# A 32-byte pad in place of a 160-byte one between the two stacks of on-chip buffers, in a decoder layer on one core

## The chip, the core and the metric

The kernel runs on one core of one Trainium2 chip. The time is the device time of one execution in microseconds (us); lower is better. The engines are named as the profile names them: PE (TensorE, matmuls), PEld (its weight loads), DVE (VectorE), ACT (ScalarE), POOL (GpSimd) and SP (SyncE, which issues most of the DMAs).

## The reference

One layer of a hybrid decoder, for 1024 tokens of width 1024 in float32:

```python
h = rms_norm(x, norm_mix_pre[l])
proj = h @ w_in[l]                        # RWKV-7 columns | S5 input | two gates
o_rwkv = rwkv7_branch(...) @ w_branch_rwkv[l]
o_s5 = s5_branch(...) @ w_branch_s5[l]
mixed = (g_rwkv * o_rwkv + g_s5 * o_s5) @ w_out[l]
x = x + rms_norm(mixed, norm_mix_post[l])
h = rms_norm(x, norm_ffn_pre[l])
f = conv_ffn(h, ffn_w_up[l], ..., ffn_w_down[l])   # up, causal conv of width 3, gelu(gate)*val, down
x = x + rms_norm(f, norm_ffn_post[l])
```

The RWKV branch is a delta-rule recurrence over time with a data-dependent decay; the S5 branch is a diagonal complex state-space scan.

## The kernel before

Every large product is done in three matmuls of 128x512 per block of 128 inputs: each float32 operand is split into a high part rounded to fp32r and a low part (the rest), and high*high, high*low and low*high are summed. In a matmul one operand is loaded into PE as weights (128x128, PEld's rows) and the other, of 128x512, is streamed through; "moving operand" below is the streamed one. In the profile's rows a matmul is written `out<-moving,weights`. There are three places in the code that issue such triples:

- `mm3_steps` (lines 173 to 175): input projection, gates, branch projections, output projection and the first up-projection units. The weights `wh`, `wl` (or `lx`) come from `load_w`, which has ACT cast a loaded tile `wf` (line 157) and DVE subtract (line 158). The moving operands are the split activations `hh`, `hl`, in one stage `e`, in another `t`, in a third `lx`.
- `product` (lines 1344 to 1346): the up-projection of the other units, by a Winograd-Strassen scheme of seven products. The weights are `h`, `l` (tags h0 to h2, l0 to l2) and for the seventh product `w`; the moving operands are `hh`, `hl` and `t`.
- `step` in `down` (lines 1518 to 1520): the down-projection, by seven products as well, with weights `wh`, `wl` and moving operands `xh`, `xl`.

PE runs in the order in which the code is written (a manual schedule for PE); background products fill the time in which the recurrences' short matmuls wait.

**Where the tiles lie.** On-chip buffers are taken from two stacks in each partition's bytes: pools opened as usual grow from the low end, pools with `side="right"` from the high end downwards. `pad` is the first thing on the right, so its size sets where everything else on the right begins. It is written once, by POOL (line 1653), and read by nothing. Nearly all large tiles are 2048 or 4096 bytes in a partition, so that on one side they have the same remainder by 512. In the two built programs these are (bytes within a partition, the lowest tile of each row; the left pool `rk` of the recurrence is the exception, at 320):

| tiles | side, pool | address before | mod 512 | address after | mod 512 |
|---|---|---|---|---|---|
| `wh`, `wl`, `wf` of load_w | left, wp | 25792 | 192 | 25792 | 192 |
| `h`, `l` of the up-projection's products | left, upz, ups, upr | 42176 | 192 | 42176 | 192 |
| `lx` (mixing), `t` of the second half's branch and output projections (`t2`) | left, lxp, work2 | 46272 | 192 | 46272 | 192 |
| `hh`, `hl` (both halves) | right, hp0, hp1 | 163648 | 320 | 163776 | 448 |
| `w` (h3, l3) of the seventh product | right, hp1 | 175936 | 320 | 176064 | 448 |
| `t` of the up-projection (topp) | right, topp | 98112 | 320 | 98240 | 448 |
| `e` (early), and the recurrence's `ar`, `bk`, `gr`, `mt` on the right | right, early, rka | 119616 | 320 | 119744 | 448 |
| `wh`, `wl`, `xh`, `xl`, `A`, `T` of the down-projection | right, dq0, dqf, dqt | 108352 | 320 | 108480 | 448 |
| `st`, `S`, `B` of the down-projection | left, dqs, dqa, dqb | 25792 | 192 | 25792 | 192 |

So before the change a right tile of the table lies 128 bytes off a left one, modulo 512 as modulo 256; after it, 256 bytes off modulo 512, and not at all modulo 256. 660 of the 2316 buffers are on the right.

Of the kernel before, what the change touches and what calls it, by code (L numbers as in the profile page):

```python
# [9 lines left out]
F32 = mybir.dt.float32  # L10
# [61 lines left out]
class Kern:  # L72
# [1558 lines left out]
    def build(self):  # L1631
        tc, nc = self.tc, self.nc
        with tc.tile_pool(name="const", bufs=1) as self.const, tc.tile_pool(name="small", bufs=1) as self.small, \
                tc.tile_pool(name="dram", bufs=1, space=DRAM) as self.dram:
            def dr(n, shape=(128, T)):
                return self.dram.tile(list(shape), F32, name=n)
            for n in ("TZ", "TA", "TG"):
                setattr(self, n, [dr(f"{n}{p}") for p in range(4)])
            self.GT = [dr(f"GT{m}") for m in range(16)]
            self.RKV = [dr(f"RKV{m}") for m in range(12)]  # L1640

            self.US = [dr(f"US{m}", (8, 16, 8, 128)) for m in range(4)]
            self.YU = [dr(f"YU{m}", (8, 16, 8, 128)) for m in range(4)]
            self.YR = [dr(f"YR{m}") for m in range(4)]
            self.X1 = dr("X1", (D, T))
            self.H0 = [dr(f"H0{k}", (128, 512)) for k in range(NK)]
            self.ACT = [dr(f"ACT{i}") for i in range(FT)]
            self.tail = self.flip = False
            psum = dict(bufs=1, space=PSUM)
            with tc.manual_schedule(engines={mybir.EngineType.PE}), \  # L1650
                    tc.tile_pool(name="pad", bufs=1, side="right") as pad:

                self.nc.gpsimd.memset(pad.tile([128, 40], F32, name="pad"), 0.0)
                with tc.tile_pool(name="hp0", bufs=1, side="right") as hp0, \
                        tc.tile_pool(name="hp1", bufs=1, side="right") as hp1, ExitStack() as tops:
                    self.hp = (hp0, hp1)
                    with ExitStack() as low:
                        self.wp = low.enter_context(tc.tile_pool(name="wp", bufs=1))
                        self.front_half()
                        self.tail = True  # L1660
                        self.ps = tops.enter_context(tc.tile_pool(name="psd", **psum))
                        self.nrm = low.enter_context(tc.tile_pool(name="nrm", bufs=1))
                        mx = []
                        with tc.tile_pool(name="work2", bufs=NT2B) as self.work:
                            self.mix_out(mx)
                        self.early_stack.close()
                        self.topp = tops.enter_context(tc.tile_pool(name="topp", bufs=1, side="right"))
                        self.y1p = low.enter_context(tc.tile_pool(name="y1p", bufs=1))
                        self.work = low.enter_context(tc.tile_pool(name="work3", bufs=NT2C))
                        self.y1, self.T = [None] * NK, [[] for _ in range(4)]  # L1670
                        self.fill, self.fill_prio = [self.first_units(0)], 0
                        self.drive([(HP2, self.mid_norms(1, mx))])
                        self.drain()
                        for j, _ in enumerate(self.parts(self.first_units(1), 4)):
                            self.prep_t(j)
                        begun = {}
                        for i in (NFIRST, NFIRST + 1):
                            wh, wl = self.load_w(self.a["w_up"][i])
                            begun[i] = self.begin(i, {n + 1: ((wh[n], wl[n]), 0) for n in range(2)})
                    with tc.tile_pool(name="upz", bufs=1) as upz, tc.tile_pool(name="ups", bufs=1) as ups, \  # L1680
                            tc.tile_pool(name="upr", bufs=1) as upr, tc.tile_pool(name="upy", bufs=1) as upy:
                        self.up = dict(zg=upz, zv=upz, h0=upz, s=ups, h1=ups, l1=ups, h2=ups, l2=ups, r1=upr, r2=upr,
                                       l0=upr, y=upy)
                        self.fast_up(begun)
                with ExitStack() as st:
                    def pool(n, **k):
                        return st.enter_context(tc.tile_pool(name=n, bufs=1, **k))
                    right = [pool(n, side="right") for n in ("dq0", "dqf", "dqt")]
                    left = [pool(n) for n in ("dqa", "dqs", "dqb")]
                    self.ps = pool("psw", space=PSUM)  # L1690
                    self.down(*right, *left)
# [212 lines left out]
```

## Time and profile before

| | |
|---|---|
| time, median of 3 runs | 1575.57 us (1574.95 to 1576.25) |
| the profiled execution's own time | 1576.7 us |
| its span, first to last instruction | 1574.9 us |
| PE busy | 1502.9 us, 95% of the span |
| DVE, ACT, POOL busy | 1127.4, 693.7, 165.5 us |
| mean granted TensorE clock | 0.98 |
| chain of work that ended last, by engine | PE 73%, DVE 14%, DMA 6%, issue 3%, ACT 3% |

PE's rows overlap each other: the end of a matmul is modelled, and the next one starts before it. How long a matmul keeps PE is therefore read from one start to the next, or from a stretch that PE fills wholly: its length by the number of weight loads in it, since each matmul has one.

### The profile page before, as it was taken

Reading aid. Unit: us, or ns where it says so; the run is one execution under the profiler, and the core shown is the slowest. Engines: PE = TensorE matmul, PEld = TensorE weight load, DVE = VectorE, ACT = ScalarE, POOL = GpSimd, SP = SyncE. Lnnn points to the kernel's source line nnn. Section 1 sums busy time; section 2 is a strip of 40 time slices with the busy share of each in tenths; the row PEclk is TensorE's granted clock in tenths of the full one; section 3 lists DMA queues with packets and bytes.
Section 4 is the critical chain, followed back from the end, with each engine's and each line's share of the span. In section 5 each row is a group of like instructions: output and inputs, shape, how many; then the busy total and the mean of one; then the engine's idle time right before and its main releaser. Section 6 shows DMA issues by size and latency. Waiting matters only on the chain.

```text
span 1574.9 us, 26064 instructions
## 1 busy us (share of the span) xinstructions
PE 1502.9 (95%) x10028; PEld 1193.0 (76%) x10028; DVE 1127.4 (72%) x1963; ACT 693.7 (44%) x1115; POOL 165.5 (11%) x218
## 2 busy tenths in 40 slices
PE   5999899999999999999998999999999999999995
PEld 4787788787777776667686888788888887888884
DVE  6798784664465666875586689877777777688777
ACT  5354442324243445554434445444444445443451
POOL 2120000515224132100000000000000000000000
PEclk9999999999999999999898999999999999999997
DMA  6164243344335256542764443322222224953722
GB/s 209 41 192 132 85 124 122 113 137 143 107 118 159 86 180 160 154 150 101 235 215 152 140 143 132 114 80 81 81 80 81 81 81 169 323 196 120 232 77 107
DMA packets 133421, 213.86 MB, mean 136 GB/s; under 512 B 38656, under 2 KB 44800, under 8 KB 133296
## 3 DMA queue, kind: packets, MB, share of 16 engines
q1 hardware_dynamic: 124208, 188.32, 36.1%
q0 software_dynamic: 7936, 21.77, 4.7%
q10 hardware_dynamic: 1152, 2.10, 0.3%
q8 instruction: 79, 1.29, 0.3%
q14 instruction: 46, 0.38, 0.1%
HBM read 156.56 MB, written 53.48 MB: 133 GB/s over the span
## 4 chain that ended last, share of the span: by engine, by line
PE 73%; DVE 14%; DMA 6%; issue 3%; ACT 3%; SPq 0%; POOL 0%; DVEq 0%; ACTq 0%; POOLq 0%
PE gm L173 10%; PE gm L174 9%; PE gm L175 9%; PE rp L1344 4%; PE rp L1345 4%; PE rp L1346 4%; DMA st<-in_w_down_dram 2%; PE mm L1346 2%; PE mm L1345 2%; PE mm L1344 2%; PE d L1519 2%; PE d L1520 2%; PE d L1518 2%; PE ch L173 2%; PE ch L174 2%
## 5 line engine op out<-in xcount | busy, mean ns | idle before, releaser
L173 PE MATMUL gm<-hh,wh 128*128 128x512 f32 x688 | 295.0, 429 | 5.3 <-ACT hh L227 2.1
L174 PE MATMUL gm<-hl,wh 128*128 128x512 f32 x688 | 273.6, 398 | 0.4 <-DVE hl L228 0.4
L175 PE MATMUL gm<-hh,wl 128*128 128x512 f32 x656 | 260.5, 397 | 0.0
L157 ACT CAST wh<-wf 128x512 fp32r<-128x512 f32 x179 | 110.6, 618 | 216.2 <-PE gm L174 131.0
L158 DVE TENSOR_TENSOR wl<-wf,wh 128x512 fp32r<-128x512 f32 x175 | 123.6, 707 | 102.8 <-ACT wh L157 95.4
L173 PEld LDWEIGHTS gm<-hh,wh 128*128 128x128 f32 x688 | 130.5, 190 | 43.6 <-issue 4.6
L174 PEld LDWEIGHTS gm<-hl,wh 128*128 128x128 f32 x688 | 131.5, 191 | 24.9 <-issue 1.4
L175 PEld LDWEIGHTS gm<-hh,wl 128*128 128x128 f32 x656 | 124.7, 190 | 29.6
L1518 PE MATMUL d<-xh,wh 128*128 128x512 f32 x308 | 120.8, 392 | 2.1 <-ACT xh L227 2.1
L1519 PE MATMUL d<-xl,wh 128*128 128x512 f32 x308 | 120.8, 392 | 1.9 <-DVE xl L228 1.9
L1520 PE MATMUL d<-xh,wl 128*128 128x512 f32 x308 | 120.5, 391 | 0.0
L1344 PE MATMUL rp<-t,h 128*128 128x512 f32 x216 | 85.5, 396 | 1.4 <-ACT p L1358 1.4
L1346 PE MATMUL rp<-t,l 128*128 128x512 f32 x216 | 85.3, 395 | 0.3 <-DVE l L228 0.3
L1345 PE MATMUL rp<-t,h 128*128 128x512 f32 x216 | 85.4, 395 | 0.0
L1519 PEld LDWEIGHTS d<-xl,wh 128*128 128x128 f32 x308 | 58.2, 189 | 15.1 <-DVE xl L228 3.2
L1518 PEld LDWEIGHTS d<-xh,wh 128*128 128x128 f32 x308 | 58.2, 189 | 14.6 <-ACT xh L227 2.4
L1520 PEld LDWEIGHTS d<-xh,wl 128*128 128x128 f32 x308 | 58.2, 189 | 12.2
L227 ACT CAST h<-r 128x1024 fp32r<-128x1024 f32 x34 | 35.7, 1050 | 63.4 <-PE rp L1345 33.9
L228 DVE TENSOR_TENSOR l<-r,h 128x1024 fp32r<-128x1024 f32 x34 | 41.7, 1225 | 30.3 <-ACT h L227 28.9
L1365 DVE SCALAR_TENSOR_TENSOR y<-zv,vecs,y 128x1023 f32<-128x1023 f32 (+1 forms) x36 | 46.1, 1280 | 8.6 <-ACT y L1363 8.6
L1358 ACT COPY p<-rp 128x512 f32<-128x512 f32 x54 | 31.4, 582 | 41.4 <-PE rp L1346 39.8
L1344 PEld LDWEIGHTS rp<-t,h 128*128 128x128 f32 x216 | 40.6, 188 | 11.5 <-ACT p L1358 2.2
(442 smaller groups left out, 3388.6 us busy)
## 6 DMA issues: line engine op xcount, KB each, us to landing
r<-in_w_up_dram SPq DMA_DIRECT2D x36, 512.0 KB, 3.2
wf<-in_w_in_dram SPq DMA_DIRECT2D x68, 256.0 KB, 2.7
st<-in_w_down_dram SPq DMA_DIRECT2D x55, 256.0 KB, 4.0
st<-ACT SPq DMA_DIRECT2D x44, 256.0 KB, 4.4
wf<-in_w_up_dram SPq DMA_DIRECT2D x36, 256.0 KB, 2.8
ACT<-y POOLq DMA_DIRECT2D x18, 512.0 KB, 2.9
GT<-ev SPq DMA_DIRECT2D x32, 256.0 KB, 2.1
wf<-in_w_br_dram SPq DMA_DIRECT2D x32, 256.0 KB, 3.2
```

Source lines behind the costliest of these rows:

```text
L157: nc.scalar.copy(h[:, :n], f[:, :n])
L158: nc.vector.tensor_tensor(l[:, :n], f[:, :n], h[:, :n].bitcast(F32), ALU.subtract)
L173: mm(ps, a, xh[k], start=k == 0, stop=False)
L174: mm(ps, a, xl[k], start=False, stop=False)
L175: mm(ps, b, xh[k], start=False, stop=k == n - 1)
L1344: mm(ps, wh[:, c], xh, start=first and k == 0, stop=False, skip_group_check=True)
L1345: mm(ps, wh[:, c], xl, start=False, stop=False, skip_group_check=True)
L1346: mm(ps, wl[:, c], xh, start=False, stop=k == 3, skip_group_check=True)
L1365: V.scalar_tensor_tensor(y[:, lag:], z[:, 0:1024 - lag], self.vec(nme, i), y[:, lag:], ALU.mult, ALU.add)
L1518: mm(ps, wh[:, c], xh[:, x], start=start, stop=False, skip_group_check=True)
L1519: mm(ps, wh[:, c], xl[:, x], start=False, stop=False, skip_group_check=True)
L1520: mm(ps, wl[:, c], xh[:, x], start=False, stop=stop, skip_group_check=True)
```

## The change

The pad is taken with 8 float32 values in each partition, not 40. Every tile on the right then lies 128 bytes higher; the left ones stay. The instructions of PE, DVE, ACT and SP stand in the same order with the same shapes in both built programs; on POOL one row differs, the memset of the pad, which is 128x8 in place of 128x40.

```diff
                     tc.tile_pool(name="pad", bufs=1, side="right") as pad:
 
-                self.nc.gpsimd.memset(pad.tile([128, 40], F32, name="pad"), 0.0)
+                self.nc.gpsimd.memset(pad.tile([128, 8], F32, name="pad"), 0.0)
                 with tc.tile_pool(name="hp0", bufs=1, side="right") as hp0, \
                         tc.tile_pool(name="hp1", bufs=1, side="right") as hp1, ExitStack() as tops:
```

## The prediction

> **What bounds the kernel now.** I read the page first, for who is on the path.
>
> ```profile
> PE 1502.9 (95%) x10028; PEld 1193.0 (76%) x10028; DVE 1127.4 (72%) x1963; ACT 693.7 (44%) x1115; POOL 165.5 (11%) x218
> PE 73%; DVE 14%; DMA 6%; issue 3%; ACT 3%; SPq 0%; POOL 0%; DVEq 0%; ACTq 0%; POOLq 0%
> PE gm L173 10%; PE gm L174 9%; PE gm L175 9%; PE rp L1344 4%; PE rp L1345 4%; PE rp L1346 4%; DMA st<-in_w_down_dram 2%; PE mm L1346 2%; PE mm L1345 2%; PE mm L1344 2%; PE d L1519 2%; PE d L1520 2%; PE d L1518 2%; PE ch L173 2%; PE ch L174 2%
> ```
>
> PE is busy for 95% of the span and carries 73% of the chain, and what it does there is the triples of 128x512 matmuls. A move of tiles can only show if it changes what one such matmul takes, or a transfer. So the next view is busy time by stretch, for stretches that PE fills wholly with one kind of triple: their length by the number of weight loads (the second x) is the time of one matmul. I chose them from the timeline, each from the start of one matmul to the start of another. The columns are PE, PEld, DVE, ACT, POOL, then the granted clock, the DMA share and GB/s.
>
> ```profile
> 805.23:811.35 6.12, 6.12 (x29) 5.07 (x27) 6.11 (x11) 2.86 (x5) 0.00 (x0) 1.00 0.58 186
> 1144.74:1161.48 16.74, 16.74 (x73) 13.57 (x72) 13.32 (x15) 6.68 (x9) 0.53 (x1) 1.00 0.25 94
> 1396.29:1401.72 5.43, 5.43 (x25) 4.50 (x24) 5.43 (x8) 3.18 (x6) 0.00 (x0) 1.00 0.64 242
> 1339.02:1341.58 2.56, 2.56 (x7) 1.98 (x6) 2.56 (x3) 0.00 (x0) 0.00 (x0) 0.50 1.03 380
> ```
>
> The first is `ch<-t,wh` and `mm<-t,wh` of lines 173 to 175, moving operand and weights both on the left: 6.12 / 27 = 226.7 ns. The second is the up-projection's `rp<-t,h` and its like, moving operand on the right, weights on the left: 16.74 / 72 = 232.5 ns. The third is the down-projection, both on the right: 5.43 / 24 = 226.3 ns. The fourth is the down-projection while the granted clock was 0.50: 2.56 / 6 = 426.7 ns, which halved is 213.3 ns.
>
> The clock was 1.00 in the first three, so it is no explanation. Nor is other work: DVE was busy for all of the two quick stretches and 13.32 of 16.74 us in the slow one. What orders the three is the distance between the two operands that PE reads at once: 0 modulo 512 in the quick ones, 128 in the slow one. Against 213.3 ns a matmul loses 13 ns in the first case and 19 in the second. I conclude that a matmul's stream and the load of the next weights hinder each other, by an amount that depends on how their addresses stand to each other. The groups by shape say the same on more instructions (the mean is of a modelled duration, so only differences count).
>
> ```profile
> L173 PE MATMUL ch<-t,wh 128*128 128x512 f32 x32 | 12.6, 392 | 0.0
> L1518 PE MATMUL d<-xh,wh 128*128 128x512 f32 x308 | 120.8, 392 | 2.1 <-ACT xh L227 2.1
> L1344 PE MATMUL rp<-t,h 128*128 128x512 f32 x216 | 85.5, 396 | 1.4 <-ACT p L1358 1.4
> ```
>
> **The change, part by part.** It removes and adds no instruction but a smaller memset, which is off the path: it runs at 3.2 us, before the first matmul's data are there, and takes 139 ns.
>
> ```profile
> L1653 POOL MEMSET pad<- x1: 139/139/139, 3.2 to 3.2; 128x40 f32 x1
> ```
>
> What it moves is the distance of each pair whose moving operand is on the right and whose weights are on the left: from 128 to 256 modulo 512, which is 0 modulo 256. Pairs on one side keep their distance. How many pairs are crossed is counted from these rows; each stands for a triple of lines of (nearly) equal count.
>
> ```profile
> L173 PE MATMUL gm<-hh,wh 128*128 128x512 f32 x688 | 295.0, 429 | 5.3 <-ACT hh L227 2.1 <-DVE last L953 1.8 <-ACT ev L1046 1.3
> L1344 PE MATMUL mm<-t,h 128*128 128x512 f32 x72 | 28.5, 395 | 0.0
> L1344 PE MATMUL rp<-hh,h 128*128 128x512 f32 x64 | 25.3, 395 | 0.0
> L1344 PE MATMUL ch<-hh,h 128*128 128x512 f32 x64 | 25.2, 394 | 0.0
> L173 PE MATMUL ch<-hh,wh 128*128 128x512 f32 x64 | 25.8, 403 | 0.0
> L173 PE MATMUL mm<-hh,wh 128*128 128x512 f32 x64 | 25.7, 402 | 0.0
> L173 PE MATMUL ch<-e,wh 128*128 128x512 f32 x32 | 14.3, 448 | 0.0
> L173 PE MATMUL mm<-e,wh 128*128 128x512 f32 x32 | 13.5, 423 | 3.4 <-ACT e L232 2.2 <-ACT et L1080 1.2
> ```
>
> With `rp<-t,h` from above: 3 x (688 + 216 + 72 + 64 + 64 + 64 + 64 + 32 + 32) = 3888 crossed matmuls.
>
> The price of one at the new distance stands in no row, since no pair of this kernel is 256 apart. The nearest rows bound it: 0 apart, 5.8 ns less (232.5 - 226.7); and, if the loss grows by the same 5.8 ns with each 128 bytes, 5.8 ns more. The only number that repeats in the rows is the remainder: distances of 0, 512, 1024 and 1536 occur within the down-projection, since a weight block lies 512 bytes after the last, and all give 226 ns. So the pattern has a period that divides 512 and is over 128: 256 or 512. I take 256, by which the new distance counts as 0, because the effect then needs one address bit fewer. That is a choice, not a finding.
>
> At 0 apart I take 5.3 ns of the 5.8, as a sequence settles only after some matmuls, and the mean durations above differ by 4. Not all of it is on the path:
>
> ```profile
> L173 PE MATMUL gm<-hh,wh 128*128 128x512 f32 x89 | 37.0, 416 | 3.5 <-ACT hh L227 2.1 <-ACT ev L1046 1.3
> L173 PE MATMUL gm<-hh,wh 128*128 128x512 f32 x363 | 161.7, 446 | 0.0
> 0.00:100.00 100.00, 81.22 (x355) 66.17 (x356) 74.37 (x237) 46.83 (x75) 17.61 (x22) 1.00 0.48 144
> 300.00:700.00 400.00, 391.77 (x4762) 289.31 (x4761) 250.80 (x610) 165.94 (x368) 103.08 (x138) 0.99 0.46 138
> 925.00:1335.00 410.00, 408.12 (x1757) 329.58 (x1756) 319.13 (x399) 203.20 (x257) 12.32 (x23) 1.00 0.26 96
> ```
>
> - Up to 100 us PE is busy for 81% only and waits for loads and the first norm: 3 x 89 = 267 crossed matmuls, counted at nothing.
> - From 300 to 700 us (the first of the two `gm` rows is that of 0 to 100 us, the second this one's) 3 x 363 = 1089 stand among the recurrence's short matmuls, so that the next weights are often a short one's: half, 1089 x 2.65 ns = 2.9 us.
> - The other 3888 - 267 - 1089 = 2532: 2532 x 5.3 ns = 13.4 us. Nearly half are in the up-projection, where PE is busy for 408 of 410 us; DVE is busy for 319 there, so it would not take over if PE took 2% less.
>
> ```profile
> L1344 PE MATMUL mm<-hh,w 128*128 128x512 f32 x72 | 28.1, 390 | 0.0
> 1161.48:1164.26 2.78, 2.78 (x14) 2.25 (x12) 1.23 (x1) 2.75 (x4) 0.00 (x0) 1.00 0.00 0
> ```
>
> - The seventh product has both operands on the right, but stands between crossed ones and so never settles: 2.78 / 12 = 231.7 ns. With quiet neighbours I give it 4 ns: 3 x 72 x 4 = 0.9 us.
>
> Together 17.2 us. Outside the up-projection PE waits now and then for DVE, DMA or ACT (23% of the chain), and a wait of fixed length there is met earlier but not shortened, while a cast that is only just in time turns into a wait. I take nine tenths: 15.5 us. The profiled execution took 1576.7 us by its own time, of which 1574.9 is the span; it becomes 1561.2, and the median of the runs shown lies 1.1 lower, so 1575.6 - 15.5 = 1560.
>
> **Transfers.** Right-side targets of DMAs move too.
>
> ```profile
> st<-in_w_down_dram SPq DMA_DIRECT2D x55, 256.0 KB, 4.0
> A<-in_w_down_dram SPq DMA_DIRECT2D x11, 256.0 KB, 5.4
> T<-ACT SPq DMA_DIRECT2D x11, 256.0 KB, 4.7
> ```
>
> `A` and `T` go from 64 past a multiple of 256 to 192 past it, where `st` has been all along, and `st` lands in 4.0 us against 5.4 and 4.7: nothing here makes 192 the worse place, and the chain names `st`. I count 0, with 1 us either way. [...]
>
> **The rivals.** *The period is 512, and 256 apart is worse* (the other side). For it: nothing excludes it, and the only step that the trace shows, from 0 to 128, is a loss. Against it: 512 needs the longer period. The place is the same crossed matmuls. With 5.8 ns more each, the same sum gives 2532 x 5.8 + 1089 x 2.9 = 17.8 us and, at nine tenths, 16 us: 1592. Slow matmuls in the present pattern last 404 ns where the usual one lasts 393; if all did, it would be 11 ns each and some 30 us, 1606, which I take as the far end. It decides as soon as 256 apart costs more than 128, thus over 232.5 ns.
>
> ```profile
> L1345 PE MATMUL rp<-t,h x216: 390/393/404, 992.9 to 1332.1; 128*128 128x512 f32 x108
> ```
>
> *No change*: any distance other than 0 modulo 512 costs the same 19 ns; or the distance is not the cause at all, and the stretches differ for a reason that goes with the stage. For it: each kind of pair occurs in stages of its own. Against it: lines 173 to 175 have both speeds with the same weights `wh`. It gives 1575.6. [...]
>
> *Half the gain*: PE gets quicker, but casts and loads that are just in time become its waits. Half of 17.2 us is 8.6: 1567. It is faster as well.
>
> **How the numbers follow.** The full gain has 0.45, half of it 0.10, no change 0.12, slower 0.33. Differences of under 0.2% (3.2 us) can hardly be told from none here. So faster 0.55, same 0.12, slower 0.33. The low end is the full sum with the interleaved matmuls at the whole price: 13.4 + 5.8 + 0.9 = 20 us, 1555. The high end reaches the middle of the slower case, 1592, which leaves out some 0.16 above and 0.03 below. The likeliest case alone spans 1555 to 1564.
>
> **What would show each step.** Right: stretches of `rp<-t,h` at 227 ns, the up-projection's 84 matmuls of one round in 19.1 us and not 19.5; `d` and `ch<-t` as before at 226 to 227; `gm<-hh,wl` and `rp<-t,h` with means lower by some 4 to 5 ns. Wrong in its choice: `rp<-t,h` at 238 ns or more, `d` unchanged. Wrong at the root: `rp<-t,h` unchanged, or `d` and `ch<-t` changed as well. Wrong in the sum: `rp<-t,h` at 227 ns, but more idle time of PE ended by `wl`, `wh` or `st`.

## The result, and the profile after

The changed kernel took 1565.05 us (median of 8 runs, 1563.06 to 1571.28) beside 1576.08 us of the kernel before in the same runs (8 runs, 1574.95 to 1579.26): a ratio of 0.9934, 95% interval 0.9915 to 0.9953, thus 11 us less. Repeated later beside other runs of before (median 1578.58) it gave 1566.99 us, ratio 0.9927 (0.9900 to 0.9954); a sixth run of that repeat, of 5725.66 us, is left out of these figures. It is faster, by seven tenths of the 15.5 us that were forecast. The profiled execution took 1569.72 us, 4.7 above the median, of which 1566.6 is the span.

From the page after, the engines' row and the two rows of the chain:

```profile
PE 1490.2 (95%) x10028; PEld 1194.1 (76%) x10028; DVE 1127.4 (72%) x1963; ACT 691.0 (44%) x1115; POOL 164.2 (10%) x218
PE 71%; DVE 14%; DMA 7%; issue 4%; ACT 3%; SPq 1%; POOL 1%; DVEq 0%; ACTq 0%; POOLq 0%
```

PE's busy time fell by 12.7 us, PE's share of the chain by two points, and DMA and issue gained one each. The next view is busy time by stretch after the change, for the same instructions as the prediction's: `ch<-t` and `mm<-t` (left, left), `rp<-t,h` (crossed), `d` (right, right), the seventh product (between crossed ones), and then the longest unbroken run of `gm`, 190 matmuls. The last row is that run before the change.

```profile
804.65:810.77 6.12, 6.12 (x28) 5.07 (x27) 6.11 (x12) 2.93 (x5) 0.00 (x0) 1.00 0.64 194
1139.24:1155.57 16.33, 16.33 (x74) 13.52 (x73) 13.32 (x15) 6.58 (x10) 0.53 (x1) 1.00 0.25 96
1386.22:1391.66 5.44, 5.44 (x25) 4.50 (x24) 5.44 (x8) 2.62 (x5) 0.00 (x0) 1.00 0.71 266
1155.57:1158.29 2.72, 2.72 (x14) 2.25 (x13) 1.22 (x1) 2.69 (x4) 0.00 (x0) 1.00 0.00 0
315.52:358.61 43.09, 43.09 (x192) 35.66 (x190) 24.58 (x77) 9.94 (x16) 6.12 (x12) 1.00 0.45 141
...
316.21:360.36 44.15, 44.15 (x191) 35.80 (x190) 24.61 (x77) 9.96 (x16) 6.70 (x13) 1.00 0.44 138
```

The crossed stretch is 16.33 us long for its 72 matmuls, 226.8 ns each where it was 232.5; `gm` went from 44.15 / 190 = 232.4 to 43.09 / 190 = 226.8; the seventh product is at 2.72 / 12 = 226.7. The two same-side stretches stayed at 6.12 us and at 5.43 and 5.44. So where PE runs on without a break, a crossed matmul became as quick as one of the same side, and those stayed as they were.

Where the time came from, and where it went again, shows when the span is cut at the same PE instructions in each profile (worked out from the starts of PE's rows). The profiles at distance 128 are before, e2 and e5 below, those at 0 modulo 256 are after, e1, the repeat e11 and e6; e5 and e6, in this order last in their cells, count up to 925 us alone, since their edit lies behind that. The last column is by how much less time all neighbouring 128x512 matmuls took after than before that ran at full clock without a gap:

| stage, us of before | at distance 128 | at 0 modulo 256 | matmuls quicker by |
|---|---|---|---|
| 0 to 100 | 100.0, 101.3, 100.4 | 98.9, 99.1, 98.2, 100.1 | 1.4 |
| 100 to 300 | 200.1, 201.4, 202.9 | 200.6, 201.0, 200.7, 200.6 | 2.5 |
| 300 to 700 | 400.1, 401.9, 399.4 | 400.2, 400.1, 399.5, 396.3 | 1.1 |
| 700 to 925 | 224.8, 222.8, 225.5 | 224.4, 224.7, 224.9, 221.8 | 2.2 |
| 925 to 1335 (up-projection) | 410.0, 410.1 | 400.8, 400.8, 401.0 | 9.6 |
| 1335 to the end | 239.9, 241.2 | 241.7, 241.8, 240.9 | 0.0 |

PE's matmuls became 16.6 us quicker, and the up-projection, where PE never waits for long, passes on 9.2 of its 9.6. Up to 925 us the matmuls are 7.1 us quicker; these stages took 925.0, 927.4 and 928.3 us at distance 128 and 924.1, 924.9, 923.3 and 918.8 at 0. The means are 4.1 us apart, but profiles of one distance differ by 3 to 6 us, so how much of the 7.1 comes through there is not settled. Before and after alone, 0.9 us, would suggest next to nothing.

Waits of PE are the first suspect: it arrives earlier and waits for the same work. Two of them, first of before, then of after, then of e2 (total us, times, longest):

```profile
PE chk L615 <- DVE t L609: 4.3, 2, 2.4
PE d L1519 <- DVE xl L228: 1.9, 3, 0.9
```

```profile
PE chk L615 <- DVE t L609: 5.9, 2, 4.0
PE d L1519 <- DVE xl L228: 3.4, 4, 1.1
```

```profile
PE chk L615 <- DVE t L609: 5.9, 2, 4.0
PE d L1519 <- DVE xl L228: 3.2, 3, 1.7
```

They are longer after the change, but as long in e2, whose matmuls are as slow as before; and in e11, the changed kernel again, the first is back at 4.3. PE's idle time in all (span less busy) was 72.0 us before and 77.0 in e2, 76.4, 76.7 and 77.5 in after, e1 and e11. So that waits take the gain is not shown. What does differ is the granted clock: inside the span it was at 0.50 for 62.1 us before and 57.1 in e2, but for 70.8, 71.3 and 71.0 us in after, e1 and e11. The part on the clock comes back to it.

### The profile page after: what moved, and what is told of

It is laid out like the page before. It is cut to its first block, busy times and chain, and to the rows that moved or that the text cites. A ratio compares the mean times of both kernels' runs of the same rounds, so it can differ in the third digit from the quotient of the medians.

```text
span 1566.6 us, 26064 instructions
## 1 busy us (share of the span) xinstructions
PE 1490.2 (95%) x10028; PEld 1194.1 (76%) x10028; DVE 1127.4 (72%) x1963; ACT 691.0 (44%) x1115; POOL 164.2 (10%) x218
## 4 chain that ended last, share of the span: by engine, by line
PE 71%; DVE 14%; DMA 7%; issue 4%; ACT 3%; SPq 1%; POOL 1%; DVEq 0%; ACTq 0%; POOLq 0%
PE gm L173 9%; PE gm L174 8%; PE gm L175 8%; PE rp L1344 4%; PE rp L1345 4%; PE rp L1346 4%; DMA st<-in_w_down_dram 2%; PE ch L173 2%; PE ch L174 2%; PE mm L174 2%; PE mm L1346 2%; PE mm L1345 2%; PE ch L175 2%; PE mm L1344 2%; PE mm L173 2%
## 5 line engine op out<-in xcount | busy, mean ns | idle before, releaser
L1346 PEld LDWEIGHTS rp<-t,l 128*128 128x128 f32 x216 | 40.5, 188 | 9.3 <-DVE l L228 1.0
```

Source lines behind the costliest of these rows:

```text
L1346: mm(ps, wl[:, c], xh, start=False, stop=k == 3, skip_group_check=True)
```

## The experiments

**Is it the distance, or the place of the right side?** e1 moves the left side instead, e2 both sides, so that the right lies where the change puts it and the distance is 128 again.

```diff
-                    tc.tile_pool(name="pad", bufs=1, side="right") as pad:
+                    tc.tile_pool(name="pad", bufs=1, side="right") as pad, tc.tile_pool(name="lpad", bufs=1) as lpad:
+                self.nc.gpsimd.memset(lpad.tile([128, 32], F32, name="lpad"), 0.0)
```

(and in e2 the pad of 8, as in the change)

> The pad stays at 160 bytes and the left side moves up by 128 bytes instead, so a right tile lies 0 bytes off a left one modulo 512 (before: 128; after: 256). Theory (the distance modulo 256 decides): crossed triples at 227 to 228 ns from start to start as in the changed kernel, the up-projection some 9 to 10 us shorter than before, the whole at 1562 to 1568 us. Rival A (the place of the right side decides, by its own addresses or by the transfers that land there; nothing on the right moves here): crossed at 232 ns, the whole at 1575 to 1577. Rival B (the period is 512, and 256 apart is only halfway): crossed at under 227 ns, the whole below 1562.

> The changed pad of 32 bytes, and the left side moved up by 128 bytes as well: the right side lies where the change puts it, but the distance is 128 again, as before. Theory (the distance decides): crossed at 232 ns, the whole at 1574 to 1578 us, the gain gone. Rival A (the right side's own place or its transfers): crossed at 227 to 228 ns, the whole at 1562 to 1568.

e1 took 1568.31 us, 0.9940 of before (0.9921 to 0.9960); e2 1577.42, 1.0005 (0.9993 to 1.0018). The crossed stretch of `rp<-t,h` in e1, then in e2:

```profile
1139.95:1156.27 16.32, 16.32 (x73) 13.52 (x72) 13.32 (x15) 6.57 (x10) 0.53 (x1) 1.00 0.26 96
```

```profile
1147.27:1164.01 16.74, 16.74 (x73) 13.57 (x72) 13.33 (x15) 6.68 (x9) 0.53 (x1) 1.00 0.27 94
```

With nothing moved on the right e1 has the change's 226.7 ns; with the right side where the change puts it e2 has the 232.5 ns of before, and the gain is gone. So rival A falls, and with it the transfers as a cause: the place of the right side by itself shows no effect here (e2's interval holds no more than 0.18%), its distance from the left has all of it. e1's distance is 0 modulo 512 and no quicker than the 256 of the change, so rival B falls too.

**Other distances.** e3 and e4 only change the pad.

```diff
-                self.nc.gpsimd.memset(pad.tile([128, 40], F32, name="pad"), 0.0)
+                self.nc.gpsimd.memset(pad.tile([128, 56], F32, name="pad"), 0.0)
```

(56 in e3, 24 in e4)

> A pad of 224 bytes: distance 64 modulo 256, which neither kernel has. Theory in its simple form (the loss grows with the distance from a multiple of 256): crossed at about 230 ns, the whole at about 1570 us. Rival C (two lines of 64 bytes behave alike within each half of the period, or the loss of 13 ns against 213 ns at distance 0 is itself a collision that another distance avoids): crossed below 226 ns, the whole below 1560, down to some 1530 if 3888 crossed matmuls lose no more than a few ns. Rival D (targets of transfers that are not at a multiple of 128 cost): crossed as the theory has it, but more idle time of PE ended by wl, wh, st or A.

> A pad of 96 bytes: distance 192 modulo 256, the mirror image of 64. Theory in its simple form (symmetric about 0): crossed at about 230 ns, the whole at about 1570 us, as with 64. Rival E (the order of the two addresses counts, the weights' load running ahead of the stream or behind it): one of 64 and 192 is quicker than 227 ns, the other slower than 230, and the two wholes differ by over 5 us.

The same stretch in e3, then in e4:

```profile
1137.19:1153.67 16.48, 16.48 (x73) 13.52 (x72) 13.33 (x15) 6.58 (x10) 0.53 (x1) 1.00 0.27 95
```

```profile
1149.06:1165.86 16.80, 16.80 (x73) 13.54 (x72) 13.33 (x15) 6.68 (x10) 0.53 (x1) 1.00 0.26 94
```

At 64 a matmul takes 228.9 ns and the whole 1568.12 us (0.9950, 0.9933 to 0.9966); at 192 it takes 233.3 ns and the whole 1580.7 (1.0020, 1.0004 to 1.0037). The two are no mirror images, as rival E has it, and the wholes differ by 12.6 us; but 228.9 ns is not under E's 227. The simple form of the theory falls. Rival D was put the wrong way round: right tiles lie 64 past a multiple of 128 before and after the change, and on a multiple of 128 only in e3 and e4. There `A` lands in 5.5 and 4.8 us and `T` in 5.1 and 5.4, beside 5.4 and 4.7 before, so their place shows no price.

**The distance by itself.**

> Leaves the layer out: one fp32r tile is streamed 48 times against the same weights, for weights that start 0, 16, 32 ... 512 bytes further on, and further out up to 1536 bytes, then 4, 8, 12 and 20 bytes; nothing else runs. Theory (the distance modulo 256 alone decides): 226 to 227 ns at 0, 256, 512, 1024 and 1536; the series repeats after 256 bytes; the values of the layer at moving minus weights of 64, 128 and 192 come back as about 230, 232 and 233 ns; nothing below 226. Rival C (the 13 ns at distance 0 over 213 are a collision that a better distance avoids): some distance at 214 to 222 ns. Rival H (the loss comes from the traffic of the other engines in the layer): 213 to 214 ns at every distance.

Its core; one PSUM tile for each offset:

```python
for i, o in enumerate(OFFS):
    ...
    for k in range(SWEEP_N):
        nc.tensor.matmul(ps, w[:, o:o + 128], m[:, 0:512], start=k == 0, stop=k == SWEEP_N - 1)
```

(`SWEEP_N` is 48; `o`, in float32 values of 4 bytes, runs through 0, 4, 8 ... 128, then 160 to 384, 1, 2, 3 and 5.) Rows of the stretches for weights 16, 32, 128, 192, 256 and 1536 bytes further on, 36 matmuls each:

```profile
22.42:30.58 8.16, 8.16 (x37) 6.76 (x36) 0.00 (x0) 0.00 (x0) 0.00 (x0) 1.00 0.01 2
33.37:41.77 8.40, 8.40 (x37) 6.76 (x36) 0.00 (x0) 0.00 (x0) 0.00 (x0) 1.00 0.00 0
100.52:108.92 8.40, 8.40 (x38) 6.76 (x36) 0.00 (x0) 0.00 (x0) 0.00 (x0) 1.00 0.00 0
145.11:153.35 8.24, 8.24 (x37) 6.76 (x36) 0.00 (x0) 0.00 (x0) 0.00 (x0) 1.00 0.01 2
189.37:197.53 8.16, 8.16 (x37) 6.76 (x36) 0.00 (x0) 0.00 (x0) 0.00 (x0) 1.00 0.00 0
433.05:441.21 8.16, 8.16 (x37) 6.76 (x36) 0.00 (x0) 0.00 (x0) 0.00 (x0) 1.00 0.01 2
```

226.7 ns at 16, 256 and 1536 bytes, 233.3 at 32 and 128, 228.9 at 192 (moving less weights: 64). The values of 16 to 240 bytes come back at 272 to 496 within 0.1 ns, and 0 and 128 differ, so the period is 256 bytes and no less. It is a comb rather than a slope: exactly 16 bytes off on either side cost nothing, 32 the whole 6.7 ns, but 4, 8, 12 and 20 bytes cost 5.6, 4.0, 3.3 and 6.7 (worked out from the starts, as the other values without a row). Nor does the distance fix the time to the last nanosecond: 128 and 384 bytes gave 233.3, 640 and 896 gave 232.4. DVE, ACT and POOL were idle, so rival H falls; and no distance tried is below 226.7, so rival C falls: with these shapes none of them gives more than the change has taken.

**Is it the reads of the load?**

> Leaves the layer out, as the distance sweep did: one fp32r tile streamed against the same weights, 48 times for each case, with 128, 96, 64 and 32 columns of weights (512 to 128 bytes read in each partition), a stream of 512, 384 and 256 columns, and weights that start 0, 64, 128 and 192 bytes further on. Theory (the loss is the load's own reads that fall together with the stream's): at distance 0 the loss over 213.3 ns goes with the columns loaded, 13.3 ns at 128, about 10 at 96, 6.7 at 64, 3.3 at 32; the same 13.3 ns stand on top of 160 and 106.7 ns for the shorter streams; the further 6 to 7 ns at 128 and 192 bytes shrink with the columns as well. Rival I (a fixed cost of issuing a matmul): 226.7 ns at distance 0 whatever the columns.

```diff
-                nc.tensor.matmul(ps, w[:, o:o + 128], m[:, 0:512], start=k == 0, stop=k == SWEEP_N - 1)
+                nc.tensor.matmul(ps[0:c, 0:n], w[:, o:o + c], m[:, 0:n], start=k == 0, stop=k == SWEEP_N - 1)
```

At distance 0 with 128, 96, 64 and 32 columns of weights under a stream of 512, then with 128 columns under a stream of 384 at distance 0, and under one of 256 at distance 0 and 128:

```profile
22.33:30.49 8.16, 8.16 (x38) 6.76 (x36) 0.00 (x0) 0.00 (x0) 0.00 (x0) 1.00 0.01 2
66.60:74.88 8.28, 8.28 (x38) 5.80 (x36) 0.00 (x0) 0.00 (x0) 0.00 (x0) 1.00 0.00 0
110.92:119.20 8.28, 8.28 (x37) 4.83 (x36) 0.00 (x0) 0.00 (x0) 0.00 (x0) 1.00 0.01 2
155.20:163.54 8.34, 8.34 (x37) 3.92 (x36) 0.00 (x0) 0.00 (x0) 0.00 (x0) 1.00 0.00 0
199.06:205.30 6.24, 6.24 (x37) 6.24 (x37) 0.00 (x0) 0.00 (x0) 0.00 (x0) 1.00 0.01 3
232.09:236.41 4.32, 4.32 (x38) 4.32 (x37) 0.00 (x0) 0.00 (x0) 0.00 (x0) 1.00 0.00 0
243.50:247.77 4.27, 4.27 (x38) 4.27 (x37) 0.00 (x0) 0.00 (x0) 0.00 (x0) 1.00 0.00 0
```

The load itself gets shorter with its columns (PEld 6.76 to 3.92 us), but the matmul does not get quicker: 226.7, 230.0, 230.0 and 231.7 ns. Neither theory foresaw that. The other half of the theory came true: under streams of 384 and 256 columns a matmul takes 173.3 and 120.0 ns at distance 0, which is 13.3 ns over three quarters and half of 213.3, as it is under 512. So at distance 0 the loss is one for each matmul, whatever the length of the stream, and it does not go with the bytes of the load. Which distance is good depends on the shapes: under 256 columns distance 128 is the quicker one (118.6 against 120.0 ns). The place of the next weights matters, then, but not through the amount that is read. What a matmul loses this time to is not settled.

**Where the rest of the gain stays.** e5 gives distance 0 to the up-projection alone, e6 to all but it.

```diff
-                    with tc.tile_pool(name="upz", bufs=1) as upz, tc.tile_pool(name="ups", bufs=1) as ups, \
+                    with tc.tile_pool(name="lpad", bufs=1) as lpad, tc.tile_pool(name="upz", bufs=1) as upz, tc.tile_pool(name="ups", bufs=1) as ups, \
...
-                        self.up = dict(zg=upz, zv=upz, h0=upz, s=ups, h1=ups, l1=ups, h2=ups, l2=ups, r1=upr, r2=upr,
+                        self.nc.gpsimd.memset(lpad.tile([128, 32], F32, name="lpad"), 0.0); self.up = dict(zg=upz, zv=upz, h0=upz, s=ups, h1=ups, l1=ups, h2=ups, l2=ups, r1=upr, r2=upr,
```

(pad 40 in e5, 8 in e6)

> The pad of before (160 bytes); only the left pools of the up-projection (h, l and their neighbours) are 128 bytes higher, so that only the up-projection's crossed triples get distance 0, and all others keep 128. Theory (each crossed matmul on PE's path gives its 4.5 to 5.5 ns, and the half-clock time of the earlier stages grows only where those are quicker): 925 to 1335 us shorter by 9 to 10 us, everything ahead of it unchanged, half-clock time as before at some 60 to 64 us, the whole 8 to 10 us below before, thus nearly all of what the change gives by itself. Rival F (the quicker up-projection is what makes the throttle take more, or its gain is lost in the down-projection): more half-clock time than before, and the whole less than 6 us below before.

> The changed pad of 32 bytes with the left pools of the up-projection 128 bytes higher: every crossed triple but the up-projection's is at 256, those of the up-projection at 128 as before. Theory (the earlier stages' 7 us of quicker matmuls are mostly given back to more half-clock time, 74 us in place of 64, and to waits): the wide matmuls up to 925 us take about 7 us less, half-clock time 70 us or more at the places of the changed kernel, the mean granted clock 0.002 to 0.003 below that of before, the whole only 1 to 4 us below before. Rival G (the lower clock of the changed kernel was chance): half-clock time as before, the clock equal to that of before within 0.001, the whole 5 to 7 us below before.

Both came out slower than before: 1585.17 us (1.0040, 1.0022 to 1.0058) and 1587.12 (1.0058, 1.0038 to 1.0078). The matmuls did what was meant, here the stretch of `rp<-t,h` in e5, then in e6:

```profile
1155.88:1172.20 16.32, 16.32 (x74) 13.52 (x72) 13.33 (x15) 6.58 (x10) 0.53 (x1) 1.00 0.29 96
```

```profile
1147.96:1164.71 16.75, 16.75 (x74) 13.57 (x73) 13.33 (x15) 6.70 (x9) 0.53 (x1) 1.00 0.26 94
```

226.7 ns in e5 and 232.6 in e6; the runs of `gm` stand the other way round. But the edit did something else as well. From e5, the view of the new tile, SP's timeline, the view of the tile `h` between 990 and 1004 us (the second of its rows is PE's wait for it, us and times), and the stretch behind it:

```profile
L1682 POOL MEMSET lpad<- x1: 125/125/125, 996.4 to 996.4; 128x32 f32 x1
...
996.94 0.33 SPq L1324 DMA_DIRECT2D r<-in_w_up_dram  x1
...
L227 ACT CAST h<-s x1: 1046/1046/1046, 1003.6 to 1003.6; 128x1024 fp32r<-128x1024 f32 x1
...
  PE rp L1344: 8.4, 1
...
1000.91:1011.15 10.24, 6.45 (x14) 4.63 (x15) 5.98 (x8) 3.07 (x4) 0.00 (x0) 0.50 0.44 158
```

PE waited 8.4 us for the first `h` and then had a granted clock of 0.50 for 10.2 us. The memset of the new tile ran at 996.4 us, after the last matmul on the old weights, and the first load of the up-projection was issued at 996.9, where before it was at 983.9 (3.3 us of these 13 stem from earlier stages). That the loads wait because tiles moved by 128 bytes each lie over two old ones is a guess that was not tried apart. By the letter e5 meets rival F, more half clock (79.4 us inside the span) and no gain, but with this late start it says nothing of F. As measures of the whole both runs are spoilt; their stages up to 925 us stand in the table above. There e6 ran at 918.8 us, 6 below before, with 30.7 us of half clock where after has 51.2, so the theory that these stages give nearly all back was not borne out by it.

**Does the clock take the gain back?** Of the 8.7 us more at half clock after the change, 6.8 lie in two stretches near 776 and 834 us. The rows show the first of them, behind the 3.4 us ahead of it; first before, then after:

```profile
772.11:775.53 3.42, 1.58 (x5) 0.78 (x5) 2.72 (x5) 1.54 (x3) 0.00 (x0) 1.00 1.02 299
775.53:785.77 10.24, 9.54 (x26) 7.11 (x25) 4.17 (x14) 1.81 (x3) 0.00 (x0) 0.50 0.61 206
```

```profile
768.71:772.10 3.39, 1.55 (x5) 0.97 (x6) 3.29 (x5) 3.23 (x6) 0.00 (x0) 1.00 0.72 191
772.12:785.78 13.66, 11.99 (x31) 8.23 (x30) 6.89 (x18) 3.01 (x5) 0.00 (x0) 0.50 0.70 221
```

In both PE was busy for under half of the 3.4 us ahead; after the change the gap came one such window earlier. e9 and e10 fill these gaps with matmuls by zeros, in the kernel before and in the changed one.

```diff
+    def dummies(self, ps, x, k, warm):
+        for _ in range(warm.get(k, 0)): self.nc.tensor.matmul(ps, self.zero, x, start=k == 0, stop=k == 0)
...
-            mm = self.nc.tensor.matmul
+            mm = self.nc.tensor.matmul; self.dummies(ps, wh[-1], k, warm)
...
+WARM0, WARM1 = {0: 6, 2: 5}, {5: 7, 6: 13, 7: 2}
```

(The last line gives the number of extra matmuls ahead of each step, in two products.)

> The kernel before, with 33 extra matmuls by weights of zeros (they add nothing to the sums) in PE's idle time ahead of five steps between 768 and 840 us, so that the windows of 3.41 us there are busy. Theory (the granted clock halves after a window in which PE was busy for under about half): the two half-clock stretches of 10 us each at 776 and 834 us go, half-clock time falls from some 62 to 42 us, and the time by 4 to 8 us, to 1570 to 1574. Rival J (the clock there follows something else, such as the load of the whole chip): half-clock time as before, time equal or up to 7 us longer.

> The changed kernel with the same 33 matmuls. Theory: the half-clock stretches of 14 us each at 772 and 830 us go, half-clock time falls from 74 to about 47 us, the time by 6 to 10 us, to 1556 to 1560; against the kernel before with the same filling the change then brings 13 to 15 us, close to the 16.6 us by which its matmuls are quicker. Rival J: no less half-clock time, time equal or longer, and 10 to 12 us between the two filled kernels as between the two unfilled ones.

> The changed kernel as it is, beside the two filled ones. Theory: 1563 to 1570 us; mean granted clock 0.001 to 0.003 below that of the kernel before in the same runs. Rival G (its lower clock was chance): the clock equal within 0.001 and the time 13 us or more below before.

From the timeline of e10, and its stretch in place of the half clock:

```profile
770.02 1.67 PE L83 MATMUL mm<-wh,zero 128*128 128x512 f32 x6 [1.76 <-ACT et L1080]
768.30:785.80 17.50, 14.63 (x68) 11.37 (x69) 12.82 (x28) 7.00 (x13) 0.00 (x0) 1.00 0.82 244
```

The half clock there is gone, and of the second stretch 3.4 us are left: inside the span it is 36.8 us in all in e10 against 71.0 in e11, and 34.3 in e9 against 62.1. So PE's gaps are what lowers the clock there. "Under about half" is not the whole rule, though: in e10 the window of 3.41 us (a third of the 10.24 above) from 767.0 us was 48% busy (worked out from PE's rows) and no half clock followed.

In its own stage, 700 to 925 us, the filling came near to what was expected of it: 221.0 us in e9 against 224.8, and 218.6 in e10 against 224.9 in e11, where the unfilled profiles above lie between 221.8 and 225.5. But on the whole e9 took 1576.7 us (0.9987 of before, 0.9969 to 1.0006) and e10 1564.92 (0.9914, 0.9891 to 0.9937), against 1578.58 and 1566.99 unfilled. The change is worth 11.8 us filled and 11.6 unfilled, not 13 to 15: as to the time, rival J was right. In these profiles other stages were longer, 100 to 300 us for one at 202.4 and 202.5 against 200.1 and 200.7; why is not shown. e10 has the lowest median of the three, but its interval overlaps that of the changed kernel's repeat, so it is not shown to be better.

The runs on record say more of the clock than the profiles, since each lists its mean. It was 0.9827 over 59 runs of before and 0.9802 over 13 of the changed kernel; e1 and e2, with the same two unused tiles and only the distance apart, have 0.9790 and 0.9831. So the lower clock is no chance (rival G falls) but goes with the distance. Within each kernel a run is some 10.9 us longer for each 0.01 by which its clock is lower (one slope fitted to the 72 runs), and at equal clock before and after lie 14.4 us apart (standard error 0.7), where their means differ by 11.7. By that the clock takes back 2.7 us. It would also explain why e3, with slower matmuls than e1 but a clock of 0.9823, is as quick on the whole. This is a correlation and not an experiment: whatever makes a run wait may lower its clock too, and the filled kernels did not gain what it promises.

## Why the prediction was right, and where it was wrong

- **The cause** (distance between moving operand and next weights): right, by e1, e2 and e7. **Period 256**: right, 226.7 ns at 0, 256, 512 and 1536 in e7, but there it was a choice that the trace could not decide, and the sign of the result hung on it; in that the prediction had luck. That addresses count at all is shown by 16.32 and 16.74 us for the same 72 matmuls in e1 and e2; a load of fewer bytes made nothing quicker in e8 (226.7 ns with 128 columns, 230.0 to 231.7 with fewer).
- **The price of 5.3 ns**: 5.7 in `rp<-t,h` and 5.6 in the long run of `gm`; the seventh product gained 5 ns where 4 were given.
- **The sum of 17.2 us on PE**: 16.6. Its parts were off both ways. Up to 100 us counted as nothing, and gave 1.4. The 1089 interleaved matmuls at half price were 2.9 and gave 1.1, nearly all of it in the one unbroken run of 190. The rest, 13.4 + 0.9 = 14.3, gave 2.5 + 2.2 + 9.6 = 14.3. The count of 3888 leaves out 32 triples (`gm<-e,wh` 16, `rp<-hh,wh` and `ch<-hh,wh` of line 1344, 8 each): 96 matmuls, 0.5 us by its price.
- **Nine tenths on the path**: this is the step that was off. 11 of 16.6 us came through, two thirds. The sentence ahead of it gave a mechanism, a wait "met earlier but not shortened"; the waits that grew after the change were as long in e2, at the old distance, so the runs do not show it. What they show in its place is a lower granted clock, which the prediction did not count at all: 71 us at half clock against 57 and 62, worth 2.7 us by the runs' mean clocks, though not proven by e9 and e10. What takes the rest, some 3 us, stays open.
- **Transfers at 0, with 1 us either way**: right, by e2. After the change `A` lands in 5.1 us against 5.4 before, `T` in 4.8 against 4.7, and `st`, which did not move, in 4.3 against 4.0 (rows below): differences of this size are none of the place's.
- **The rivals**: *period 512* and *no change* fall. *Half the gain* at 1567 describes the result better than the forecast of 1560 does: 1565.05 and, repeated, 1566.99 lie nearer to it. Its reason, casts and loads that become PE's waits, was not seen.
- **Marks in the profile**: `rp<-t,h` at 227 ns, `d` and `ch<-t` unchanged: seen. The mean of `gm<-hh,wl` was to fall by 4 to 5 ns and fell by one (397 to 396, rows below): it mixes the quicker runs with half-clock stretches and with matmuls beside gaps. The mark of a wrong sum, idle time ended by `wl`, `wh` or `st`, did not come, though the sum was too high: PE's list of waits has none of the three.

```profile
L175 PE MATMUL gm<-hh,wl 128*128 128x512 f32 x656 | 259.9, 396 | 0.0
L1344 PE MATMUL rp<-t,h 128*128 128x512 f32 x216 | 84.4, 391 | 1.4 <-ACT p L1358 1.4
...
st<-in_w_down_dram SPq DMA_DIRECT2D x55, 256.0 KB, 4.3
A<-in_w_down_dram SPq DMA_DIRECT2D x11, 256.0 KB, 5.1
T<-ACT SPq DMA_DIRECT2D x11, 256.0 KB, 4.8
```

## What to carry to other kernels

Measure a matmul from start to start in a stretch that PE fills alone, apart for each pair of buffers it reads; where two kinds differ, compare the address of the stream with that of the next weights, and move one side by an unused tile. What such a gain is worth is counted stage by stage, over several profiles of each kernel: here it passed on nearly whole where PE hardly waits (9.2 of 9.6 us, in the 410 us of which it was busy for 408 before), and elsewhere by an amount that profiles of one and the same distance, 3 to 6 us apart, could not settle. A wait that is longer in the profile after is not yet an effect of the change; e2, with the gain taken out again, had the same ones. An unused tile put in the middle of a stack that is used again can cost more than it brings, as e5 and e6 show (0.4% and 0.6% slower than before).

## What was not expected of the hardware

- Under a stream of 512 columns and 128 columns of weights no distance of the sweep gave a matmul under 226.7 ns at full clock, even with no other engine at work, while it takes 426.7 at half clock (2.56 us for 6, in the down-projection before), of which half is 213.3. Fewer columns of weights made it slower at distance 0, up to 231.7 ns.
- Ahead of 54 of the 77 half-clock stretches of nine profiles (before, after, e1 to e4, e9 to e11; 6 of 10 before, 8 of 9 after) PE had been busy for under half of one window of 3.41 us, often with no gap over 2 us (1.4 at most ahead of 775.5 us before); ahead of the one at 570.7 us after the change it had been busy for 2.73 of 3.41 us. All stretches but the last of a span were whole multiples of 3.41 us (3.41, 10.24 and 13.65 us long before and after), on one grid through each profile that lies elsewhere against the start of each span. PE need not be idle throughout ahead of one: it worked for 1.55 of the 3.39 us ahead of 772 us above.
- In the profile of e9 the granted clock had a mean of 0.940 (0.95 from 768.3 to 785.8 us and from 826.5 to 844.0), and yet the rows of `rp<-t,h` have the same mean of 396 ns as before, where the clock's was 0.980. And the run of 5725.66 us had a mean granted clock of 0.251; nothing in the other runs shows why.
